# Two-expert weighted sum on one core: the first and last tile's loads in one piece, the last tile's first products on ScalarE

## The chip, the cores and the metric

The kernel runs on 1 core of one Trainium2 chip. The metric is device time in microseconds (us) of one execution. Before the change the median of 4 runs is 241.63 us (241.57 to 241.78).

## The reference

There are 16 x 1024 = 16384 tokens. Each token has two vectors of 512 float32 values (the outputs of its two experts) and two scalar weights. The result is the weighted sum of the two vectors:

```python
def reference(expert_outputs, combine_weights):      # (16,1024,2,512), (16,1024,2)
    weights = combine_weights[..., np.newaxis]
    return np.sum(expert_outputs * weights, axis=2).astype(np.float32)
```

So 67.1 MB are read, 33.6 MB are written, and for each output value there are two multiplications and one addition.

## The kernel before

The tokens are dealt out to the 128 partitions: partition p holds 128 tokens that follow one another in memory. A tile is J = 8 tokens of every partition, so the loop at line 44 runs over 16 tiles (g = 0 to 15). For each tile there is an input tile `et` (128 partitions x 8 tokens x 1024 values, 4 MB) and an output tile `ot` (128 x 8 x 512, 2 MB). Both come from pools with 4 buffers (lines 38, 39), so at most four loads can be under way ahead of the computation, and tile g + 4 can be loaded when tile g has been computed. The weights, 256 values for each partition, are loaded once as `wt` (line 42).

For each token there are two VectorE (DVE) instructions on 128 x 512 values: line 53 multiplies the first expert's vector by its weight into `ot` (TENSOR_SCALAR), and line 56 multiplies the second expert's vector by its weight and adds what is in `ot` (SCALAR_TENSOR_TENSOR). No other engine computes.

Loads are issued by SyncE (SP, line 50) and stores by ScalarE's queue (ACT, line 64). An engine's instructions, issues of DMAs included, are executed in the order of its own queue. The framework that builds the program sets that order and the waits between engines. The order need not be that of the source: in the trace, two line 53 instructions mostly stand ahead of the two line 56 instructions of the same tokens. SP's transfers go through one DMA queue (q1 in the profile) and ACT's through another (q10). Each transfer is spread over 16 DMA engines, and each of them moves 8 packets for it, one for each of 8 partitions. A packet is as long as what the transfer moves for that partition: 4 KB for each token loaded, 2 KB for each token stored.

Fourteen of the tiles are loaded and stored whole, which makes packets of 32 KB and 16 KB. The first tile is loaded, computed and stored in pieces of 1, 1, 2 and 4 tokens, and the last one in pieces of 4, 2, 1 and 1 (line 35 and the loop at line 48):

```python
    parts = {0: (1, 1, 2, 4), per // J - 1: (4, 2, 1, 1)}
```

Of the kernel before, what the change touches and what calls it, by code (L numbers as in the profile page):

```python
# [1 line left out]

# [4 lines left out]


@with_exitstack
def kernel(  # L10
    ctx: ExitStack,
    tc: tile.TileContext,
    expert_outputs: bass.AP,
    combine_weights: bass.AP,
    out: bass.AP,
):


    nc = tc.nc
    b, s, k, h = expert_outputs.shape  # L20
    assert k == 2
    n = b * s
    P = nc.NUM_PARTITIONS
    per = n // P
    assert per * P == n
    eo = expert_outputs.rearrange("b s k h -> (b s) (k h)").rearrange("(p t) f -> p t f", p=P)
    cw = combine_weights.rearrange("b s k -> (b s) k").rearrange("(p t) k -> p (t k)", p=P)
    o = out.rearrange("b s h -> (b s) h").rearrange("(p t) f -> p t f", p=P)

    dt = mybir.dt.float32  # L30
    mult = mybir.AluOpType.mult
    add = mybir.AluOpType.add

    J = 8
    parts = {0: (1, 1, 2, 4), per // J - 1: (4, 2, 1, 1)}

    wpool = ctx.enter_context(tc.tile_pool(name="w", bufs=1))
    ipool = ctx.enter_context(tc.tile_pool(name="in", bufs=4))
    opool = ctx.enter_context(tc.tile_pool(name="out", bufs=4))

    wt = wpool.tile([P, per * k], dt)
    nc.scalar.dma_start(out=wt, in_=cw)

    for g in range(per // J):
        et = ipool.tile([P, J, k * h], dt)
        ot = opool.tile([P, J, h], dt)
        c0 = 0
        for c in parts.get(g, (J,)):
            t0 = g * J + c0
            nc.sync.dma_start(out=et[:, c0 : c0 + c, :], in_=eo[:, t0 : t0 + c, :])  # L50
            for i in range(c0, c0 + c):
                t = g * J + i
                nc.vector.tensor_scalar_mul(  # L53
                    out=ot[:, i, :], in0=et[:, i, 0:h], scalar1=wt[:, 2 * t : 2 * t + 1]
                )
                nc.vector.scalar_tensor_tensor(  # L56
                    out=ot[:, i, :],
                    in0=et[:, i, h : 2 * h],
                    scalar=wt[:, 2 * t + 1 : 2 * t + 2],
                    in1=ot[:, i, :],  # L60
                    op0=mult,
                    op1=add,
                )
            nc.scalar.dma_start(out=o[:, t0 : t0 + c, :], in_=ot[:, c0 : c0 + c, :])
            c0 += c


# [1 line left out]
_INS = ['expert_outputs', 'combine_weights']  # L69
_OUTS = [((16, 1024, 512), 'float32')]  # L70


# [23 lines left out]
```

## Time and profile before

| | before |
|---|---|
| median of 4 runs | 241.63 us |
| the profiled execution's own time | 241.38 us |
| its span in the profile | 239.6 us |
| DVE busy | 137.5 us (57%), 256 instructions |
| DMA moved | 100.81 MB, mean 421 GB/s |
| loads (q1) and stores (q10) | 65.5% and 33.1% of the 16 engines' span |

The profile is of one execution. Its span is the time from the program's first instruction to its last. The execution's own time is 1.78 us longer than the span, and it lies 0.25 us below the median of the runs. Of the engines that compute, the table shows how long they were busy. Of the DMA queues it shows how long their packets took, as a share of 16 engines over the whole span, so that 100% would mean that every DMA engine had a packet in hand all the time.

### The profile page before, as it was taken

How to read it: one execution, taken by the hardware profiler on the slowest of the kernel's cores; microseconds unless marked ns; L12 is line 12 of the kernel's file. 1: busy time of each engine (PE TensorE's matmuls, PEld its weight loads, DVE VectorE, ACT ScalarE, POOL GpSimd, SP SyncE). 2: the span in 40 equal slices, each digit the busy share in tenths (PEclk: the TensorE clock that was granted, in tenths of full speed). 3: DMA queues.
4: the chain of work that ended last, by engine and by line, in shares of the span. 5: the costliest groups of instructions: out<-in, count | busy, mean ns of one | idle time of the engine just before them, and what ended most of it. 6: DMA issues, size and time to landing. Idle time of an engine off the chain costs nothing.

```text
span 239.6 us, 392 instructions
## 1 busy us (share of the span) xinstructions
DVE 137.5 (57%) x256; POOL 0.2 (0%) x4
## 2 busy tenths in 40 slices
DVE  1570969392763909458093672917639095597303
POOL 0000000000000000000000000000000000000000
DMA  7999999999999999999999999999999999999995
GB/s 259 436 423 469 405 470 404 417 409 424 451 413 432 451 438 413 446 435 413 429 451 418 429 454 438 413 428 449 416 432 446 438 413 443 416 421 438 423 423 205
DMA packets 6482, 100.81 MB, mean 421 GB/s; under 512 B 720, under 2 KB 848, under 8 KB 2128
## 3 DMA queue, kind: packets, MB, share of 16 engines
q1 hardware_dynamic: 3168, 67.11, 65.5%
q10 hardware_dynamic: 3312, 33.69, 33.1%
q14 instruction: 2, 0.02, 0.0%
HBM read 67.24 MB, written 33.55 MB: 421 GB/s over the span
## 4 chain that ended last, share of the span: by engine, by line
DMA 86%; DVE 11%; issue 1%; SPq 0%; DVEq 0%
DMA et<-in_expert_outputs_dram 69%; DMA out_dram<-ot 18%; DVE ot L56 6%; DVE ot L53 4%; SPq L50 0%; DVEq L91 0%
## 5 line engine op out<-in xcount | busy, mean ns | idle before, releaser
L53 DVE TENSOR_SCALAR ot<-et,wt 128x512 f32<-128x512 f32 x128 | 56.3, 481 | 98.9 <-DMA et<-in_expert_outputs_dram 94.0
L56 DVE SCALAR_TENSOR_TENSOR ot<-et,wt,ot 128x512 f32<-128x512 f32 x128 | 90.2, 745 | 0.1
L80 POOL MEMSET const-uint8-127<- 128x1 uint8 x1 | 0.1, 103 | 0.0
L80 POOL MEMSET const-bfloat16-1.0<- 128x1 bf16 x1 | 0.1, 102 | 0.0
L80 POOL MEMSET const-float32-0.0<- 128x1 f32 x1 | 0.1, 99 | 0.2 <-issue 0.2
L80 POOL MEMSET const-float32-1.0<- 128x1 f32 x1 | 0.1, 99 | 0.0
## 6 DMA issues: line engine op xcount, KB each, us to landing
et<-in_expert_outputs_dram SPq DMA_DIRECT2D x14, 4096.0 KB, 49.2
out_dram<-ot ACTq DMA_DIRECT2D x14, 2048.0 KB, 41.2
et<-in_expert_outputs_dram SPq DMA_DIRECT2D x2, 2048.0 KB, 28.2
et<-in_expert_outputs_dram SPq DMA_DIRECT2D x4, 512.0 KB, 17.4
et<-in_expert_outputs_dram SPq DMA_DIRECT2D x2, 1024.0 KB, 15.5
out_dram<-ot ACTq DMA_DIRECT2D x2, 1024.0 KB, 25.0
out_dram<-ot ACTq DMA_DIRECT2D x4, 256.0 KB, 7.3
out_dram<-ot ACTq DMA_DIRECT2D x2, 512.0 KB, 20.2
```

The costliest lines, as they stand in the source:

```text
L53: nc.vector.tensor_scalar_mul(out=ot[:, i, :], in0=et[:, i, 0:h], scalar1=wt[:, 2 * t : 2 * t + 1])
L56: nc.vector.scalar_tensor_tensor(out=ot[:, i, :], in0=et[:, i, h : 2 * h], scalar=wt[:, 2 * t + 1 : 2 * t + 2], in1=ot[:, i, :], op0=mult, ...
L80: nc = _bacc.Bacc("TRN2", target_bir_lowering=False, num_devices=1)
```

## The change

The two tiles in pieces go. Every load is one transfer of 8 tokens. The stores of all tiles but the last are whole too, and the last tile is computed whole as to its load, but stored in pieces of 4, 2 and 2 tokens. In the last tile the first product of each token is made by ScalarE, as an activation that copies with a scale (the weight, a value for each partition), in place of VectorE's TENSOR_SCALAR. The second product with the addition stays on VectorE.

```diff
-    parts = {0: (1, 1, 2, 4), per // J - 1: (4, 2, 1, 1)}
+    copy = mybir.ActivationFunctionType.Copy
+    last = per // J - 1
...
         et = ipool.tile([P, J, k * h], dt)
         ot = opool.tile([P, J, h], dt)
+        nc.sync.dma_start(out=et, in_=eo[:, g * J : (g + 1) * J, :])
         c0 = 0
-        for c in parts.get(g, (J,)):
-            t0 = g * J + c0
-            nc.sync.dma_start(out=et[:, c0 : c0 + c, :], in_=eo[:, t0 : t0 + c, :])
+        for c in (4, 2, 2) if g == last else (J,):
             for i in range(c0, c0 + c):
                 t = g * J + i
-                nc.vector.tensor_scalar_mul(
-                    out=ot[:, i, :], in0=et[:, i, 0:h], scalar1=wt[:, 2 * t : 2 * t + 1]
-                )
+                w0, w1 = wt[:, 2 * t : 2 * t + 1], wt[:, 2 * t + 1 : 2 * t + 2]
+                if g == last:
+                    nc.scalar.activation(out=ot[:, i, :], in_=et[:, i, 0:h], func=copy, scale=w0)
+                else:
+                    nc.vector.tensor_scalar_mul(out=ot[:, i, :], in0=et[:, i, 0:h], scalar1=w0)
                 nc.vector.scalar_tensor_tensor(
...
-            nc.scalar.dma_start(out=o[:, t0 : t0 + c, :], in_=ot[:, c0 : c0 + c, :])
+            nc.scalar.dma_start(
+                out=o[:, g * J + c0 : g * J + c0 + c, :], in_=ot[:, c0 : c0 + c, :]
+            )
             c0 += c
```

More of the change, by code (lines that the diff above doesn't have):

```diff
@@ L58 @@
                     in0=et[:, i, h : 2 * h],
-                    scalar=wt[:, 2 * t + 1 : 2 * t + 2],
+                    scalar=w1,
                     in1=ot[:, i, :],
```

## The prediction

> **What bounds the kernel now.** I read the page first: the engines' shares, the DMA queues, then the chain that ended last.
>
> ```profile
> DVE 137.5 (57%) x256; POOL 0.2 (0%) x4
> ...
> q1 hardware_dynamic: 3168, 67.11, 65.5%
> q10 hardware_dynamic: 3312, 33.69, 33.1%
> ...
> DMA 86%; DVE 11%; issue 1%; SPq 0%; DVEq 0%
> ...
> L53 DVE TENSOR_SCALAR ot<-et,wt 128x512 f32<-128x512 f32 x128 | 56.3, 481 | 98.9 <-DMA et<-in_expert_outputs_dram 94.0
> L56 DVE SCALAR_TENSOR_TENSOR ot<-et,wt,ot 128x512 f32<-128x512 f32 x128 | 90.2, 745 | 0.1
> ...
> out_dram<-ot ACTq DMA_DIRECT2D x14, 2048.0 KB, 41.2
> ```
>
> Packets of the two queues fill 98.6% of the 16 DMA engines' span, and DVE waits 94 us for loads. So only two things can save time: fewer microseconds of packets, or less idle DMA time at the two ends. To find that idle time I asked for the DMA share by stretches (last two columns: DMA share, GB/s).
>
> ```profile
> 0.00:1.70 1.70, 0.00 (x0) 0.20 (x4) 1.00 0.00 0
> 1.70:20.00 18.30, 8.91 (x16) 0.00 (x0) 1.00 1.04 426
> ...
> 120.00:200.00 80.00, 49.88 (x95) 0.00 (x0) 1.00 1.01 433
> 200.00:228.00 28.00, 15.75 (x30) 0.00 (x0) 1.00 1.00 427
> 228.00:235.00 7.00, 0.80 (x2) 0.00 (x0) 1.00 0.98 411
> 235.00:236.70 1.70, 1.49 (x3) 0.00 (x0) 1.00 0.21 84
> 236.70:238.20 1.50, 0.00 (x0) 0.00 (x0) 1.00 0.94 350
> 238.20:239.60 1.40, 0.00 (x0) 0.00 (x0) 1.00 0.00 0
> ```
>
> The first 1.7 us and the last 1.4 us have no data at all: fixed ends that the change doesn't touch. Between them there is one hole, 1.34 us wide (79% of 1.7). The timeline shows what stands there.
>
> ```profile
> 192.12 0.88 DVE L53 TENSOR_SCALAR ot<-et,wt 128x512 f32<-128x512 f32 x2 [5.91 <-DMA et<-in_expert_outputs_dram]
> ...
> 206.65 0.88 DVE L53 TENSOR_SCALAR ot<-et,wt 128x512 f32<-128x512 f32 x2 [5.98 <-DMA et<-in_expert_outputs_dram]
> ...
> 229.78 0.48 DVE L53 TENSOR_SCALAR ot<-et,wt 128x512 f32<-128x512 f32 x1 [3.90 <-DMA et<-in_expert_outputs_dram]
> 234.68 0.48 DVE L53 TENSOR_SCALAR ot<-et,wt 128x512 f32<-128x512 f32 x1 [4.42 <-DMA et<-in_expert_outputs_dram]
> 235.09 1.41 DVE L56 SCALAR_TENSOR_TENSOR ot<-et,wt,ot 128x512 f32<-128x512 f32 x2
> ```
>
> The last token's load lands at 234.66. Everything else has left the queues by then, so the DMA engines wait for three DVE instructions. But not all of them wait. In the trace's packet records the completion packets of the third-last store stand at 235.11 to 235.65 on 15 engines and at 236.69 on the sixteenth. This engine has been some 1.2 us late since about 165 us (a store's last completion packet moves from 168.64 to 169.80, after an 8 KB packet of queue q14, the instructions', at 159.87). It has no gap: at 236.70 it goes on with the next store. **So the hole is real on 15 engines and free: the sixteenth is busy until 238.06, and the program ends with it.**
>
> **Step 1, fewer small packets.** From the packet records, one packet of 32, 16, 8, 4, 2 KB takes 1213, 611, 309, 159, 84 ns. On one engine the next starts 4 ns before the end (155 apart for 4 KB), for 2 KB none. A tile loaded in pieces costs each partition 155 + 155 + 306 + 607 = 1223 ns, a whole one 1209. With 8 partitions per engine and two tiles that is 14 x 8 x 2 = 0.22 us. Stores in pieces cost 84 + 84 + 155 + 306 = 629 against 607: 22 x 8 x 2 = 0.35 us, less the new last tile's 306 + 155 + 155 = 616, so 9 x 8 = 0.07 us back. Ten transfers fewer (45 to 35) save ten completion packets, 6 ns each: 0.06 us. **Sum: 0.56 us on every engine.** It counts in full, as the late engine has no gap. The Trainium skill ("DMA: Bandwidth & Descriptors", rules for kernel authors) asks for 1 MiB or more per DMA, and its fit (for DMAs issued from GpSimd) has a fixed cost near 2 us each. By that the six loads saved would be worth some 12 us. The stretch 1.7 to 20 us, where they are queued, moves 426 GB/s against 433 later, so the trace shows almost none of it.
>
> **Step 2, the start.** Nothing is stored until tile 0 is whole. Loads start at 1.74; the weights (8 x 46 ns) and slow first packets put their effective start at 2.36. A whole tile is 14.55 us (192.12 to 206.65), by bytes 9.70 for the load and 4.85 for the store. Load 0 ends at 12.1, is seen 0.6 later, DVE takes 8.6 us (34.83 to 43.41 in a whole tile), the store's first packet follows its issue by 0.84 (235.86 to 236.70): 22.1 us. Four loads (38.8 us) are queued meanwhile, so no DMA engine idles: cost 0. If four were not enough, each us would cost one. What changes is how far loads run ahead: 2.04 loads without a store. After that the queues alternate packet by packet (eight load and eight store packets per tile, hence 14.55).
>
> **Step 3, the end.** This is what decides. The last load's packets end at E = 2.36 + 16 x 9.70 + 13.96 x 4.85, about 225.3. By then 13.96 stores have moved, so 1.04 stores (5.0 us of packets) are still queued on each engine. They cover the last tile's computation, which before had nothing to cover it. From E, the mean over the engines, to the computation's start is 1.2 us (packet records 205.4, timeline 206.65). Then come one first product, four line 56 at 0.66 start to start (2.73 in all) and hand-overs (0.1). No ACT computation is in the trace: I bound one product by the nearest rows, 0.48 (the same operation on DVE) and 0.745 (DVE with two inputs), and take 0.745, the dearer, as it is a different engine. The first piece is issued at E + 4.8, its packets start at E + 5.6. The other engines have run dry at E + 5.0 and lose 0.6; the late one is busy until E + 6.3 and loses nothing, 0.7 us to spare. Pieces two and three need DVE until E + 7.4, which 2.45 us of packets of piece one cover, provided ACT makes its products ahead of the store issues. That is likely: ACT has all eight ready at once, and DVE's queue shows that what is ready goes first.
>
> **Sum.** The late engine ends at 238.06 - 0.56 = 237.50, the others at about 237.1 (235.4 in the mean at that third-last store, 1.35 of packets after it, less 0.56, plus 0.6 lost, plus 0.3 of spread); with completion and the fixed end (1.38) the span is 238.9 instead of 239.6: **-0.7 us**. The profiled execution (241.38) lies 0.25 under the median, so the same difference is put on 241.63: **240.9 us**.
>
> **Rivals.**
> *ACT keeps the written order.* Then each piece's products stand behind the store before it, which waits for DVE: pieces two and three each take 0.35 (store issue) + 0.745 + 1.41 + 0.1 = 2.6 us after the one before. The last piece's packets start at E + 10.8 and end at E + 12.0, where the forecast has E + 11.3. The gain is gone: 241.5. For it speaks that an engine's queue is in order; against it DVE's reordered queue.
> *ACT starts slowly (the other side).* ACT has computed nothing before the last tile. A one-time start-up x between the load's landing and its first product delays all pieces; 0.7 us are free, the rest is added to the end, and from x = 1.9 us the kernel is slower. From the rows, x lies between 0.06 (ACT's first DMA issue takes 0.40, later ones 0.34) and 4.1 (its load of the weights, issue to landing). I take none in the forecast: ACT is idle for 6 us before load 15, so a start-up that needs no data hides there. If it stands behind the load's wait, half of 4.1 gives 2.05 - 0.7 - 0.7: 242.3; all of it 244.3.
> The Trainium skill ("ScalarE: Activation LUTs", what ACT_TABLE_LOAD costs) has about 2.7 us for a switch of the function table, and its rules send multiplications to VectorE; no run here shows either, and by it this rival would be 242.9.
> *ACT's products too early in its queue*, ahead of stores 13 and 14. The 229.78 row shows such a case: one token's product ahead of the previous token's line 56, which then waited 4.4 us for a load. Here stores would wait for load 15, and after E the DMA engines would idle about 7 us: 246 to 247.
> *The late engine isn't late this time.* Then the others decide (237.1 + 1.38 = 238.5): 240.5.
>
> **Chances.** Forecast 0.48, no late engine 0.06, written order 0.22, slow start 0.17, too early 0.04, anything else 0.03. A measurement here can tell about 0.2% (0.48 us) from no change: faster is below 241.15, slower above 242.11. The forecast is 0.25 us beyond that line, so a quarter of it falls to "same". Faster: 0.36 + 0.06 + 0.04 = 0.46. Same: most of written order, that quarter, and a start-up under 1.9 us, 0.34. Slower: 0.20. The range runs from the case without a late engine to half the slow start, 240.3 to 242.3; it leaves out 0.15.
>
> **What would show it.** Step 1: q1's and q10's summed packet time falls by about 0.5 us. Step 2: DMA share near 1.0 from 1.7 us on, DVE's first instruction near 12.7, no store packet before 22. Step 3: load 15 seen near 226.5; no SP or DVE wait on a store; the DMA share stays high until about 1.4 us before the end. Wrong if ACT's first product starts over 0.7 us after the load, if the store queue is empty when load 15 lands, or if load-only or store-only stretches move less than 430 GB/s.

## The result and the profile after

The changed kernel takes 241.34 us (median of 53 runs, 241.09 to 242.01); the kernel before took 241.66 us beside it (78 runs, 241.11 to 243.04). **The ratio is 0.9984, 95% interval 0.9977 to 0.9990: 0.39 us faster.** (The ratios here aren't quotients of the two medians and can differ from them by about 0.001.) The forecast was 240.9 against 241.63, so the sign is right and the gain about half of the one forecast.

The profiled execution of the changed kernel took 241.43 us with a span of 239.64; that of before took 241.38 with 239.60. The one lies 0.09 above its median and the other 0.28 below, so this pair of traces shows where time moved, but not the net gain. The page of the changed kernel, with lines that answer to those of before and three for ScalarE and the weights:

```profile
DVE 133.8 (56%) x248; ACT 6.4 (3%) x9; POOL 0.2 (0%) x4
...
q1 hardware_dynamic: 2304, 67.11, 65.5%
q10 hardware_dynamic: 2736, 33.69, 33.0%
...
L57 DVE TENSOR_SCALAR ot<-et,wt 128x512 f32<-128x512 f32 x120 | 52.6, 480 | 92.9 <-DMA et<-in_expert_outputs_dram 79.0
...
L55 ACT ACT_TABLE_LOAD x1 | 1.3, 1283 | 227.3 <-DMA out_dram<-ot 227.3
L55 ACT ACTIVATE ot<-et,wt 128x512 f32<-128x512 f32 x8 | 5.1, 710 | 1.5 <-DVE ot L58 1.5
...
out_dram<-ot ACTq DMA_DIRECT2D x15, 2048.0 KB, 25.5
...
wt<-in_combine_weights_dram ACTq DMA_DIRECT2D x1, 128.0 KB, 13.2
```

The bound is the same: loads and stores fill 98.5% of the DMA engines' span, and VectorE waits 79 us for loads. New are a load of ScalarE's function table (1.28 us, once), eight products of 710 ns, and 13.2 us until the weights have landed, where it was 4.1. Their 1 KB packets now take turns with 32 KB packets of loads. A whole store lands 25.5 us after its issue in the median, where it was 41.2: fewer stores are left over in the queue behind the loads.

The stretches of the changed kernel (start and end, length, busy time and count of DVE, ACT and POOL, clock, DMA share, GB/s):

```profile
1.70:3.00 1.30, 0.00 (x0) 0.00 (x0) 0.00 (x0) 1.00 1.41 403
3.00:13.00 10.00, 0.00 (x0) 0.00 (x0) 0.00 (x0) 1.00 0.97 412
...
20.00:40.00 20.00, 13.39 (x26) 0.00 (x0) 0.00 (x0) 1.00 0.99 410
40.00:120.00 80.00, 49.00 (x92) 0.00 (x0) 0.00 (x0) 1.00 1.00 432
...
228.00:231.50 3.50, 2.16 (x4) 3.49 (x6) 0.00 (x0) 1.00 0.96 412
231.50:233.00 1.50, 1.50 (x3) 0.87 (x2) 0.00 (x0) 1.00 0.27 115
```

The kernel before, in the first four of these stretches (no ACT column):

```profile
1.70:3.00 1.30, 0.00 (x0) 0.00 (x0) 1.00 0.88 211
3.00:13.00 10.00, 4.59 (x8) 0.00 (x0) 1.00 1.03 427
...
20.00:40.00 20.00, 13.73 (x27) 0.00 (x0) 1.00 1.01 431
40.00:120.00 80.00, 46.95 (x88) 0.00 (x0) 1.00 1.00 428
```

Two things are to be seen. The hole at the end is still there, 1.1 us wide (73% of 1.5) where it was 1.3; it now stands ahead of the last tile's stores. And bytes are lost early: 410 against 431 GB/s in the twenty microseconds in which the first large stores join the loads. The kernel before loses some later (428 against 432 GB/s from 40 to 120 us), but less. The rows from 1.7 to 13 us are harder to compare, as these views count a whole packet where it starts: the changed kernel has 403 against 211 GB/s in the first, because its first packets are larger, and 412 against 427 in the second. What stands in the hole is in the timeline of the changed kernel (start, length, engine, line, operation, count, and in brackets the idle time before it and what ended it):

```profile
227.29 1.28 ACT L55 ACT_TABLE_LOAD   x1 [227.29 <-DMA out_dram<-ot]
228.59 3.78 ACT L55 ACTIVATE ot<-et,wt 128x512 f32<-128x512 f32 x6
...
232.11 1.66 ACTq L66 DMA_DIRECT2D out_dram<-ot  x2
233.82 1.33 ACT L55 ACTIVATE ot<-et,wt 128x512 f32<-128x512 f32 x2 [1.46 <-DVE ot L58]
...
236.02 0.34 ACTq L66 DMA_DIRECT2D out_dram<-ot  x1
```

Load 15 is seen at 227.2. The table load stands behind that wait, so ScalarE's first product starts 1.3 us later, and the first piece is issued at 232.11. Six products run ahead of the pieces' stores, the last two behind the second store (issued 233.44). The first piece's own packets follow 0.84 us after its issue. In the packet records 15 DMA engines have no packet for 1.06 us on average before the first piece's packets. The sixteenth finishes store 14 at 233.42, after that piece was ready, and goes on without a gap: its share of the three pieces ends at 235.87, 237.12 and 238.37. The program ends with it.

### The profile page after: what moved, and what is told of

The parts are those of the page before. It is cut to its first block, busy times and chain, and to the rows that moved or that the text cites. A ratio compares the mean times of both kernels' runs of the same rounds, so it can differ in the third digit from the quotient of the medians.

```text
span 239.6 us, 377 instructions
## 1 busy us (share of the span) xinstructions
DVE 133.8 (56%) x248; ACT 6.4 (3%) x9; POOL 0.2 (0%) x4
## 4 chain that ended last, share of the span: by engine, by line
DMA 65%; DVE 22%; another core or an unknown queue 8%; issue 1%; ACT 1%; SPq 0%; DVEq 0%; ACTq 0%
DMA et<-in_expert_outputs_dram 56%; DVE ot L58 14%; DMA out_dram<-ot 9%; DVE ot L57 8%; ACT ot L55 1%; ACT L55 1%; SPq L48 0%; DVEq L95 0%; ACTq L66 0%; DVEq L57 0%
## 5 line engine op out<-in xcount | busy, mean ns | idle before, releaser
L57 DVE TENSOR_SCALAR ot<-et,wt 128x512 f32<-128x512 f32 x120 | 52.6, 480 | 92.9 <-DMA et<-in_expert_outputs_dram 79.0
L55 ACT ACT_TABLE_LOAD x1 | 1.3, 1283 | 227.3 <-DMA out_dram<-ot 227.3
L55 ACT ACTIVATE ot<-et,wt 128x512 f32<-128x512 f32 x8 | 5.1, 710 | 1.5 <-DVE ot L58 1.5
## 6 DMA issues: line engine op xcount, KB each, us to landing
out_dram<-ot ACTq DMA_DIRECT2D x15, 2048.0 KB, 25.5
wt<-in_combine_weights_dram ACTq DMA_DIRECT2D x1, 128.0 KB, 13.2
```

The lines of the kernel that those rows point to most:

```text
L55: nc.scalar.activation(out=ot[:, i, :], in_=et[:, i, 0:h], func=copy, scale=w0)
L57: nc.vector.tensor_scalar_mul(out=ot[:, i, :], in0=et[:, i, 0:h], scalar1=w0)
```

## The experiments

**Theory A**, from this trace: the end is set by the one late DMA engine, which has no gap. What delays the last tile's computation (the table load, ScalarE's order) is free as long as stores that are still queued cover it, and the missing half of the gain went at the start. **Its rivals:** the table load and the hole cost the missing time; or ScalarE's products earn what was gained, and the whole loads nothing. All times are medians, and each ratio is against the kernel before on the same chip (runs 1 to 4, 5 to 8 and 9 to 11 share one each). The intervals of the ratios reach 0.0009 to 0.0018 to either side, so smaller differences between runs can't be told.

**1. Table load out of the tail.** The changed kernel, and a product of one value per partition at the start:

```diff
     nc.scalar.dma_start(out=wt, in_=cw)
+    warm = wpool.tile([P, 1], dt)
+    nc.gpsimd.memset(warm, 0.0)
+    nc.scalar.activation(out=warm, in_=warm, func=copy, scale=1.0)
```

> The changed kernel with one more ScalarE activation on a 128x1 scratch tile right after the weights' issue, so that the function table is loaded at the start. Theory A (the one late DMA engine sets the end; in the changed kernel it had no gap, only the other 15 had one of 1.06 us): ACT_TABLE_LOAD leaves the tail, the first piece is issued 1.28 us sooner, the hole on the 15 engines shrinks to 0.1 us or so, and the end moves by 0.2 us at most: 241.1 to 241.4. Theory B (the hole in the tail sets the end): about 1.0 us faster, 240.3.

Measured: 241.46 us, ratio 0.9986 (0.9977 to 0.9995), 0.06 over theory A's range and far from theory B's. Its timeline and two of its stretches (columns as above):

```profile
227.25 3.78 ACT L58 ACTIVATE ot<-et,wt 128x512 f32<-128x512 f32 x6 [224.59 <-DMA out_dram<-ot]
...
230.78 1.66 ACTq L69 DMA_DIRECT2D out_dram<-ot  x2
```

```profile
231.50:233.00 1.50, 0.57 (x1) 0.51 (x1) 0.00 (x0) 1.00 0.98 410
...
237.70:238.20 0.50, 0.00 (x0) 0.00 (x0) 0.00 (x0) 1.00 0.06 25
```

Every piece is issued 1.3 us earlier and the hole is gone (0.98 instead of 0.27). Fifteen engines end by 237.7. But 0.06 is one engine of 16, and that one is busy until 238.3, as in the changed kernel (238.38). The time doesn't move: 1.28 us on the computation's path was free.

**2. The last tile's products on VectorE**, all else as in the changed kernel:

```diff
-                if g == last:
-                    nc.scalar.activation(out=ot[:, i, :], in_=et[:, i, 0:h], func=copy, scale=w0)
-                else:
-                    nc.vector.tensor_scalar_mul(out=ot[:, i, :], in0=et[:, i, 0:h], scalar1=w0)
+                nc.vector.tensor_scalar_mul(out=ot[:, i, :], in0=et[:, i, 0:h], scalar1=w0)
```

> The changed kernel with the last tile's first products back on VectorE; loads whole, stores of the last tile in 4, 2, 2. DVE alone makes the pieces ready about 4.3, 6.5 and 8.6 us after the load is seen, the changed kernel 4.9, 6.2 and 8.8. Theory A: same as the changed kernel within 0.15 us, 241.2 to 241.5. Theory B: 0.2 to 0.6 us faster, as the first piece comes sooner: 240.8 to 241.1. Theory C (ScalarE's share is what brought the gain): at or above the time before, 241.7 to 242.3.

Measured: 241.58 us, 0.9989 (0.9979 to 0.9999), 0.08 over theory A's range, which can't be told from the changed kernel. The pieces are issued at 232.12, 234.23 and 236.35, within 0.8 us of the other order. The ScalarE part of the change brings nothing that these runs can see.

**3. The first tile in pieces again**, loads and stores, with the end as changed:

```diff
-        nc.sync.dma_start(out=et, in_=eo[:, g * J : (g + 1) * J, :])
         c0 = 0
-        for c in (4, 2, 2) if g == last else (J,):
+        for c in {0: (1, 1, 2, 4), last: (4, 2, 2)}.get(g, (J,)):
+            if g == 0:
+                nc.sync.dma_start(out=et[:, c0 : c0 + c, :], in_=eo[:, c0 : c0 + c, :])
+            elif c0 == 0:
+                nc.sync.dma_start(out=et, in_=eo[:, g * J : (g + 1) * J, :])
```

> The changed kernel with the first tile loaded, computed and stored in pieces of 1, 1, 2, 4 as before. Stores lag further behind loads (about 2.9 tiles in place of 1.04), so the last tile's computation is covered entirely. Theory A: the dearer first packets of a whole first load go (0.4 us or so), 0.28 us of small packets come back, the late engine sets the end: 241.0 to 241.3. Theory B: the tail's hole goes, 1.0 us faster than the changed kernel: 240.2 to 240.5.

Measured: 241.15 us, 0.9977 (0.9966 to 0.9987). Load 15 is seen at 222.3, five microseconds sooner than in the changed kernel, the first piece is issued at 227.11, and there is no hole:

```profile
231.50:233.00 1.50, 0.00 (x0) 0.00 (x0) 0.00 (x0) 1.00 0.98 415
```

**4. The other half of the change alone**: the first tile whole, the last one in pieces of 4, 2, 1 and 1 as before, all on VectorE (by run 2's edit, not shown again):

```diff
-        nc.sync.dma_start(out=et, in_=eo[:, g * J : (g + 1) * J, :])
         c0 = 0
-        for c in (4, 2, 2) if g == last else (J,):
+        for c in (4, 2, 1, 1) if g == last else (J,):
+            nc.sync.dma_start(out=et[:, c0 : c0 + c, :], in_=eo[:, g * J + c0 : g * J + c0 + c, :])
...
```

> The first tile whole as in the changed kernel, the last tile loaded and stored in 4, 2, 1, 1 on VectorE as before. Theory A: 0.28 us of small packets are saved and the whole first load costs 0.4 us or more at the start: 241.6 to 241.9, about as before. If the start is where the change gains: 241.2 to 241.4, as the changed kernel.

Measured: 243.5 us, 1.0068 (1.0055 to 1.0080). **This was a miss**: half of the change alone costs 1.8 us. Its timeline and stretches (DVE, POOL):

```profile
236.88 0.49 DVE L54 TENSOR_SCALAR ot<-et,wt 128x512 f32<-128x512 f32 x1 [2.29 <-DMA et<-in_expert_outputs_dram]
```

```profile
235.10:236.60 1.50, 0.00 (x0) 0.00 (x0) 1.00 0.36 145
236.90:237.90 1.00, 1.00 (x2) 0.00 (x0) 1.00 0.00 0
```

The last token's load lands at 236.85, where the kernel before had 234.66, and all 16 engines, the late one too, have nothing to move (0.00) while VectorE computes that token. The start part has delayed the loads against the stores, and nothing covers the tail.

**5. The changed kernel once more**, beside runs 6, 7 and 8 on their chip.

> The changed kernel again, on the same chip as the next three, to compare them with. Both theories: 0.998 to 0.999 of the time before, 241.2 to 241.4.

Measured: 241.47 us, 0.9984 (0.9970 to 0.9997), the first result again.

**6. Runs 1 and 3 together**: first tile in pieces, table load at the start.

> First tile in pieces of 1, 1, 2, 4, the rest as changed, and the function table loaded at the start. Theory A: with 2.9 tiles of stores queued the table load was covered already, and the late engine sets the end: as start_pieces alone, 0.997 to 0.9985 of the time before, 240.9 to 241.2. If the table load still costs there: 1.0 us less, 240.2.

Measured: 241.21 us, 0.9976 (0.9964 to 0.9988). One stretch (DVE, ACT, POOL):

```profile
236.90:237.90 1.00, 0.00 (x0) 0.00 (x0) 0.00 (x0) 1.00 0.06 25
```

The engines other than the late one end by 236.8 and the late one at 237.90: with the cover and the early table load both there, the late engine is still what ends.

**7. Fewer VectorE instructions.** If the late engine is late because of instruction fetches (queue q14), then moving instructions from VectorE must move the fetches. Run 6 with every tile's first products on ScalarE:

```diff
-                if g == last:
-                    nc.scalar.activation(out=ot[:, i, :], in_=et[:, i, 0:h], func=copy, scale=w0)
-                else:
-                    nc.vector.tensor_scalar_mul(out=ot[:, i, :], in0=et[:, i, 0:h], scalar1=w0)
+                nc.scalar.activation(out=ot[:, i, :], in_=et[:, i, 0:h], func=copy, scale=w0)
```

> As e6, with the first products of all 16 tiles on ScalarE: 128 instructions leave DVE, so its queue of about 165 ends before the place (about its 190th instruction) where the second instruction fetch came; ScalarE's queue is as short. Theory A (a fetch on queue q14 makes one DMA engine 0.84 us late, and the second one, at 160 to 173 us, is what makes the late engine): the engines end together, 0.4 to 0.8 us sooner than e6, 240.2 to 240.7. If the late engine has another cause: as e6 within 0.15 us, as DVE was never the limit.

Measured: **240.46 us, 0.9941 (0.9924 to 0.9959)**, the fastest of all. The page and one stretch (DVE, ACT, POOL):

```profile
DVE 86.6 (36%) x128; ACT 82.1 (34%) x130; POOL 0.3 (0%) x5
```

```profile
236.90:237.90 1.00, 0.00 (x0) 0.00 (x0) 0.00 (x0) 1.00 0.02 8
```

The time is in theory A's range, but a step of its reasoning failed: one fetch was expected, and there are still two, now at 72.0 and 94.5 us (run 6: 44.1 and 160.0). The latest engine is 0.8 us behind the mean of the others (237.30 against 236.53) instead of 1.4 (237.90 against 236.48). That is 0.6 of the 0.75 us between the medians of runs 6 and 7; the rest lies outside the profiled span (see Step 2 below). The size of the lag fits one fetch on that engine instead of two.

**8. More VectorE instructions.** Run 1, with ten settings of one unused value per partition ahead of each of 15 tiles:

```diff
+    idle = wpool.tile([P, 1], dt)
...
+        if g != last:
+            for _ in range(10):
+                nc.vector.memset(idle, 0.0)
```

> The changed kernel with the table loaded at the start, and ten memsets of a 128x1 scratch tile on DVE in front of each of the first 15 tiles: 150 instructions of some 0.06 us, 0.6 to 1 us a tile where DVE is idle for 6. DVE's queue grows to about 415, so there should be a third fetch. Theory A, if the fetches meet the same DMA engine: 0.8 us slower than the preloaded kernel, 242.2; if they meet different engines: no more than 0.2 us. If fetches don't matter: within 0.15 us, 241.3 to 241.5.

Measured: 242.09 us, 1.0008 (0.9995 to 1.0021), 0.6 us over run 1 and over run 5 on the same chip. Its page:

```profile
DVE 142.4 (59%) x398; ACT 6.6 (3%) x10; POOL 0.3 (0%) x5
...
q14 instruction: 3, 0.02, 0.0%
```

A third fetch, at 10.3, 42.5 and 137.9 us. After the last of them one engine completes its part of a load at 169.69, 1.55 us behind the fifteenth of the 16 (168.15). The program's last packet ends at 238.91, against 238.32 in run 1. The direction is as expected; the size is under the expected 0.8.

**9. Only the first tile's loads in pieces**, its store whole:

```diff
-        nc.sync.dma_start(out=et, in_=eo[:, g * J : (g + 1) * J, :])
+        l0 = 0
+        for c in (1, 1, 2, 4) if g == 0 else (J,):
+            nc.sync.dma_start(
+                out=et[:, l0 : l0 + c, :], in_=eo[:, g * J + l0 : g * J + l0 + c, :]
+            )
+            l0 += c
```

> The changed kernel with only the loads of tile 0 in pieces of 1, 1, 2, 4; its store stays whole. The first packets get cheaper (0.4 us at most), but store 0 is issued some 4.3 us sooner, so 0.44 of a tile fewer stores are queued when the last load ends. Theory A (that queue covers the last tile's computation): 2.15 us of cover go, all 16 engines run dry before the first piece, the end comes 1.3 us or so later than the changed kernel: 242.4 to 242.9. If only the first packets' cost counts: 240.9 to 241.2.

Measured: 242.27 us, 1.0019 (1.0003 to 1.0035), just under theory A's range. Its timeline and one stretch:

```profile
223.76 1.28 ACT L60 ACT_TABLE_LOAD   x1 [223.76 <-DVE ot L63]
229.22 3.78 ACT L60 ACTIVATE ot<-et,wt 128x512 f32<-128x512 f32 x6 [4.18 <-DMA et<-in_expert_outputs_dram]
```

```profile
231.50:233.00 1.50, 1.50 (x3) 1.50 (x3) 0.00 (x0) 1.00 0.16 66
```

The first store is issued at 18.40 instead of 22.52, so more stores have moved when the last load ends: load 15 is seen at 229.2, 2.0 us later than in the changed kernel, and by so much fewer stores are left to cover the computation. Though the table load is ahead of the wait here, even the late engine runs dry (at 233.46, and the first piece's packets start about 233.6). That is the point at which the computation begins to cost.

**10. Run 4 with the first tile's store in pieces too:**

```diff
-        for c in (4, 2, 1, 1) if g == last else (J,):
-            nc.sync.dma_start(out=et[:, c0 : c0 + c, :], in_=eo[:, g * J + c0 : g * J + c0 + c, :])
+        if g < last:
+            nc.sync.dma_start(out=et, in_=eo[:, g * J : (g + 1) * J, :])
+        for c in {0: (1, 1, 2, 4), last: (4, 2, 1, 1)}.get(g, (J,)):
+            if g == last:
+                nc.sync.dma_start(
+                    out=et[:, c0 : c0 + c, :], in_=eo[:, g * J + c0 : g * J + c0 + c, :]
+                )
```

> As e4 (first tile loaded whole, last tile loaded and stored in 4, 2, 1, 1 on VectorE), with the stores of tile 0 in pieces of 1, 1, 2, 4. Each small store packet lets a 32 KB load packet pass, so loads run three tiles further ahead, about as before the change. Theory A (e4 lost its 1.8 us because too few stores were queued for the small last loads to take turns with): back to about the time before, 241.4 to 241.9. If the whole first load itself is what cost e4: 243.3 to 243.6 again.

Measured: 240.96 us, 0.9963 (0.9949 to 0.9976): 2.5 us off run 4, more than expected, by four small stores 220 us ahead of the end. The timeline and one stretch (DVE, POOL):

```profile
230.94 0.49 DVE L59 TENSOR_SCALAR ot<-et,wt 128x512 f32<-128x512 f32 x1 [5.62 <-DMA et<-in_expert_outputs_dram]
```

```profile
235.10:236.60 1.50, 0.00 (x0) 0.00 (x0) 1.00 0.98 385
```

The last token's load lands at 230.9 instead of 236.85, and the DMA engines are full where run 4 had 0.36. The queues take turns packet by packet. Tile 0 is now stored in 32 packets of 2 to 8 KB per engine instead of 8 of 16 KB, and each lets a 32 KB packet of loads pass, so the loads get ahead and stores are left over for the end.

This run shows a second thing. But for its whole first load this kernel does what the kernel before does, and it takes 240.96 us where that took 241.65 on the same chip. A whole first load alone gains 0.7 us; it is the whole first store that costs.

**11. The end alone**: the kernel before, with only the last tile changed (loaded whole, stored in 4, 2, 2), all on VectorE. It is run 3 with run 2's edit.

> Before, with only the last tile changed: loaded whole, stored in 4, 2, 2, all of it on VectorE. Against e3 this takes away ScalarE's part alone, where 2.9 tiles of stores cover the tail. Theory A: as e3, 241.0 to 241.3. If ScalarE's products bring something: 241.5 or more.

Measured: **240.81 us, 0.9961 (0.9947 to 0.9975)**, better than expected. Its timeline:

```profile
222.01 0.88 DVE L57 TENSOR_SCALAR ot<-et,wt 128x512 f32<-128x512 f32 x2 [5.97 <-DMA et<-in_expert_outputs_dram]
...
226.36 4.57 ACTq L66 DMA_DIRECT2D out_dram<-ot  x3
```

All three pieces are issued by 230.6, while the engines have packets until 236.2 to 236.8 (the late one until 238.1). So VectorE's 8.6 us of last-tile work, from 222.01 on, are hidden.

## Why the prediction was right in sign and too large

**Step 1 (fewer small packets, 0.56 us on every engine): half of it came.** Summed packet time per engine fell from 156.99 to 156.97 us for loads and from 79.27 to 79.00 for stores, 0.29 in all. The stores' 0.27 are what their terms said (0.28). The loads' 0.22 came as 0.02 in this pair, because other load packets became longer, as the next point says. How much varies: runs 1, 2 and 8 have the same loads and 156.53 to 156.68.

**Step 2 (the start costs 0): this is the term that was mis-sized.** No DMA engine idles for want of queued loads, as forecast. But time went to longer packets. I counted the bytes moved up to a moment from the packet records, each packet's spread over its time, and took what is missing against 433 GB/s (32 KB in 1.209 us on each of 16 engines). The changed kernel is behind the one before by 0.16 us at 3.6 us, 0.09 at 20 us, 0.41 at 60 us and 0.36 at 215 us. By the first tile's part of Step 1 it should be 0.3 ahead there, so 0.7 us are missing. A small part goes at the very start: the step took the slow first packets of before over unchanged, but with a whole first load they are 32 KB packets, and most of the first 16 take 1.8 to 2.0 us instead of 1.21. The larger part goes where the first large stores join the loads: from 23.5 to 26.9 us, 25 load packets of the changed kernel take up to 2.07 us, 0.7 us per engine in sum. In the kernel before there are 45 such packets from 39 to 59 us, 0.4 us per engine in sum.

The other traces say which half of the first tile this goes with. At 60 us the five kernels with its load and store in pieces have 3.45 to 3.56 us missing (before, runs 3, 6, 7, 11), and run 10 with only the load whole has 3.53. The six with both whole have 3.68 to 3.86 (the changed one, runs 1, 2, 4, 5, 8), and run 9 with only the store whole has 3.97. So the loss goes with the whole first store and not with the whole first load. Each of these is a single execution.

Three pairs with the same end measure load and store together as time: run 3 against the changed kernel 0.0007, run 6 against run 1 0.0010, run 11 against run 2 0.0028 of the time, or 0.17, 0.24 and 0.68 us in favour of the pieces. Single pairs are within their intervals; all three have the same sign. Some of the scatter lies outside the profiled span: run 3's time is 2.13 us longer than its span in the median and run 6's 1.93, where all the others have 1.76 to 1.81. By median spans the three pairs give 0.6, 0.4 and 0.75 us. Why runs 3 and 6 have more outside it isn't known.

Within the step, store 0 came 1.2 us later than worked out (issued at 22.52, not 21.3), since load 0 ended at 12.83, not 12.1, and the weights landed only at 13.91 (4.83 before).

**Step 3 (the end): the mechanism held.** The queued stores cover the last tile's computation on the late engine, and that engine sets the end: in run 1 the others end 1.2 us sooner and the time is the same. Load 15's packets end at 225.54 in the mean (forecast 225.3), but that is luck: two errors cancel. Only 13.7 stores had moved by then and not 13.96, by which the step's formula gives 224.0, and 1.5 us of long packets and gaps, which the formula doesn't have, came on top. Two more sizes were off and all but cancel. The cover was about 6.3 us instead of 5.0, because the stores started 1.2 us later: piece one's packets start at 232.95 (232.11 + 0.84), 15 engines have been idle for 1.06 by then, so the queue ran out at 231.9, which is 6.3 after 225.54. And ScalarE's table load took 1.28 us that the step had put at 0. The 15 engines' 1.06 us of idle time instead of 0.6 is the landing: load 15 is seen 1.66 us after the mean of the packets' ends, not 1.2. In this profiled execution the late engine's end is 238.37, 0.87 over the forecast 237.50. Of this, 0.7 is the time missing in Step 2; the rest isn't traced.

**The hole of before** wasn't quite free. The prediction lets the program end with the sixteenth engine at 238.06, but in the trace of before all 16 end between 238.07 and 238.22: the hole had used up what the others had to spare. So 0.16 of the forecast 0.7 us, from 238.22 down to 238.06, came from no term of the sum. Run 10, which has no such hole, ends with its late engine at 238.06 too, and the others 1.2 us sooner. Its trace is 0.36 us shorter than that of before and its median 0.7; the rest of this difference isn't traced.

**Rivals.** *ACT keeps the written order* was half true: products 7 and 8 stand behind the second store, and the third piece's packets start at about 236.86, 0.26 us before the late engine is through with piece two. It cost nothing, by this small margin, and run 2 shows no gain without it. The prediction's price for it doesn't follow: it sets the end at E + 12.0 against E + 11.3, but the late engine's 237.50 of the Sum is E + 12.2, so by the Sum the written order is free. *ACT starts slowly* happened, with x = 1.28, under the 1.9 from which the kernel would have been slower. By the prediction's own signs that counted against it (a first product over 0.7 us after the load; it came after 1.4), but run 1 took the start-up away and gained nothing. The Trainium skill ("ScalarE: Activation LUTs", what ACT_TABLE_LOAD costs) gives 1283 ns for the load and 1380 ns more for a drain behind it, for every switch to another table set. The load takes the same 1283 ns in the profile rows above. The drain doesn't show for this first load: in the records the load ends at 228.573 and the first product starts at 228.585. *No late engine* wasn't seen in any trace of the changed kernel. Run 7 has the least late one, but it is another kernel, and that its 240.46 is near this rival's 240.5 says little. *ACT's products too early* didn't occur and wasn't run.

**What the change is worth by its parts.** By the ratios the end alone (run 11) gains 0.9 us, or 0.6 with the products on ScalarE (run 3); the median spans of these two agree within 0.1 us, so the difference lies outside the span. The whole first tile takes back 0.2 to 0.7, and beside that most of the cover: with it load 15 lands some 5 us later (227.2 against 222.0 to 222.3). Run 4 and run 9 show what that is worth where there is less of it to spare. A version that beats both kernels is run 11, the old start with the new end, and better still run 7, which adds ScalarE's products in all tiles. Not run is what run 10 points to: the first load whole, its store in pieces, and the new end.

**Open.** The packet records name a queue and not the DMA engine, so that both fetches meet one engine is inferred. Run 6 shows it best: the latest engine's stores complete 0.14 us behind the next engine's at 40 us, 0.89 at 53 us and 1.66 at 170 us, with the fetches at 44.1 and 160.0. Why the first 32 KB packets and those at the first large stores are slow wasn't tried, nor what spreads single executions of the changed kernel over 0.9 us.

## What to carry to other kernels

Where DMA fills the span, the tail's computation is free as long as stores are still queued when the last load lands, and this cover is set at the start: small stores there let large loads pass, whole ones let stores draw level. So move one end at a time and test each half alone. By the ratios the new end was worth -0.9 us here, the whole first tile +1.6, and the two together -0.4; and of the first tile the whole load alone was worth -0.9 (run 10). And before shortening the tail, look for the one DMA engine that ends last: with 15 of 16 engines waiting, most of the hole that the mean share shows isn't worth anything (run 1).

## What the runs showed of the hardware

An instruction fetch costs data time. Each is one 8 KB packet of queue q14 (309 ns), and the next 32 KB load packet takes 1744 to 1751 ns instead of 1213 in most traces: 0.31 + 0.53 = 0.84 us on one DMA engine. It isn't made up later: in the changed kernel the latest engine's stores complete 0.36 us behind the next engine's up to 173 us, and 1.20 from the fetch at 173.2 up to 218 us. Moving 120 VectorE products to ScalarE shifted the fetches and gave 0.75 us (run 7 against run 6), 0.6 of it in the span. The Trainium skill ("DMA: Bandwidth & Descriptors", queues, rings and completion order) lists row 14 as internal to the runtime and says that an engine takes turns between its queue rows by whole packets of some 9 to 17 descriptors. The traces show the turns, but one record at a time: one partition's 32 KB of a load, then one partition's 16 KB of a store. So a queue's share of the bytes follows the length of its packets, which is what runs 4 and 10 turn on.
